# A decoder trunk's attention stage: weight fetches moved a step ahead, stores and reloads on GpSimd's queue, key halves in one transfer, one projection block kept for the last norm

## The chip, the cores and the metric

The kernel runs on one core of one Trainium2 chip. The metric is the device time of one execution in microseconds, the lower the better. All inputs lie in the chip's memory (HBM) when it starts; the result is written there.

## The reference

A trunk of two layers on one sequence of 1024 tokens with 1024 channels: one mLSTM layer, then one differential-attention layer, each followed by a squared-ReLU MLP, with a final norm. The change touches only the attention layer:

```python
for blk in range(S // Q_BLOCK):                 # 8 query blocks of 128
    q0 = blk * Q_BLOCK
    kv_len = q0 + Q_BLOCK                       # causal: keys 0 .. kv_len
    s1 = einsum('bhqd,bhkd->bhqk', q1[:, :, q0:kv_len], k1[:, :, :kv_len])
    s2 = einsum('bhqd,bhkd->bhqk', q2[:, :, q0:kv_len], k2[:, :, :kv_len])
    p1 = softmax(where(mask, s1, -inf)); p2 = softmax(where(mask, s2, -inf))
    a = p1 - lam * p2
    outs.append(einsum('bhqk,bhkv->bhqv', a, v[:, :, :kv_len]))
o = concatenate(outs, axis=2)
o = rms_norm(o, subln_g, SUBLN_EPS) * (1 - lam_init)    # per head, 128 channels
x = x + g1 * (o.reshape(B, S, 1024) @ w_out)
```

There are 8 heads; each has two query and key vectors of 64 channels and one value of 128. Everything is float32; the kernel reaches that accuracy on TensorE by splitting each operand into a high and a low part (float32r) and adding three products.

## The kernel before

**Stages.** The program is straight-line. An mLSTM layer and its MLP come first; then the query and key projections (`rope_out`), which store the rotated queries to the DRAM tensor `qdr` and the keys to `kdr`, high and low parts apart. The attention stage follows, then the second half of the output projection, the second MLP and the final norm. Tokens are handled in two halves throughout: half 0 is tokens 0 to 511, half 1 the others.

**The attention stage.** A *unit* is one head and one query block. `jobs` lists runs of units: heads 0 to 4 with all 8 blocks, then heads 5, 6, 7 with blocks 0 to 3, then heads 5, 6, 7 with blocks 4 to 7. For each step `i` of the loop the program issues `scores` of unit i+2, `combine` of unit i, `values` of unit i-1, and, two steps after a head's half is complete, its `subnorm`. `scores` multiplies the queries by the keys' high part (`ka`, line 960) and low part (`kb`, line 961), adds the mask (962) and takes the exponential on ScalarE (970). `combine` forms p1 - lam p2, transposes it (987) and copies it back (988). `values` multiplies by `v` (1001).

**Loads of a job.** `load` (line 923 on) brings, for each of the head's two vectors, the queries (`q`), the keys' high part twice and the keys' low part twice: the 64 rows of a key are wanted on partitions 0 to 63 and again on 64 to 127, since the queries' high and low parts lie there one above the other. That is a loop over `dup` with two transfers of 64 rows per key tile. The tiles have two buffers each (`kp`, bufs=2), so a job's keys are loaded while the job before it is computed. `load_v` brings the values.

**Fill work.** While the attention runs, other matmuls fill TensorE. `chunks` projects the values of heads 2 to 7 in three chunks (`token_steps`, lines 253 to 269, 8 steps each, with weights `w_vb` fetched and split into high and low at the chunk's start); `v_store` copies each step's result to `sv` and stores every second step to `vdr`. `goal(i)` says how many steps must have been issued by step i. `project_a` does the output projection of half 0 in 8 blocks (weights `w_do`, residual from `xdr`), one block per loop step after the last head's half 0 is normed. The sub-norm's results go straight into `yh` and `yl` where these are free; before that they are stored to `odr` and brought back by `reload`.

**What sets the order.** A scheduler orders each engine's instructions from the program's order and its own estimate of when each can run; `tc.issue_after` adds an edge on one engine. Each engine, SP included, runs its instructions strictly in order. Every DMA of the kernel is issued on SP's queue, so a transfer there also waits for whatever the transfers ahead of it wait for.

Of the kernel before, what the change touches and what calls it, by code (L numbers as in the profile page):

```python
# [17 lines left out]
P = 128  # L18
T = 1024
D = 1024  # L20
NB = D // P
# [3 lines left out]
NC = T // P  # L25
BH, BD, BV = 8, 64, 128
# [29 lines left out]
def tile_yoco(ctx: ExitStack, tc: tile.TileContext, x, c, pos, cst, vec, bg, lp, ada,  # L56
              w_in, w_v0, w_v, w_o, w_mo, w_kv, w_vb, w_q, w_do, w_up, w_dn, out):
    nc = tc.nc
    pe, act, dve, sp = nc.tensor, nc.scalar, nc.vector, nc.sync
# [15 lines left out]
    def f32(ap):  # L75
        return ap.bitcast(F32)
# [13 lines left out]
    yh = ctile([P, 2, NB, HT], "yh", F32R)  # L90
    yl = ctile([P, 2, NB, HT], "yl", F32R)
# [5 lines left out]
    kdr = dr.tile([2, 2 * BH, BD, T], F32, tag="kdr", name="kdr")  # L97
    qdr = dr.tile([2 * BH, 2, BD, T], F32, tag="qdr", name="qdr")
    odr = dr.tile([2, BH, 2, P, HT], F32, tag="odr", name="odr")
# [74 lines left out]
    def wfetch(src, shape):  # L174
        r = wp.tile(shape, F32, tag="w", name="wraw")
        sp.dma_start(out=r, in_=src)
        return r

    def wload(src, shape, nbg=1, pool=None, r=None, hpool=None):
        if r is None:  # L180
            r = wfetch(src, shape)
        h = (pool or hpool or wp).tile(shape, F32R, tag="w", name="wh")
        l = (pool or wp).tile(shape, F32R, tag="w", name="wl")
        split(h, l, r)
        bgwork(nbg)
        return h, l
# [63 lines left out]
                        if after and idx[-1] == n - 1 and (gi, h) in after:  # L250
                            after[gi, h]()

    def token_steps(src, w, consume, nbg=1, hook=None):
        ws = [wload(src[j], [P, 4, w], nbg) for j in range(2)]
        for tb in range(NC):
            ps = gps()[:, :w]
            half, o = tb // 4, (tb % 4) * P
            for k in range(NB):
                wh, wl = ws[k // 4]
                a, b = yh[:, half, k, o:o + P], yl[:, half, k, o:o + P]  # L260
                pe.matmul(ps, lhsT=a, rhs=wh[:, k % 4], start=k == 0, stop=False)  # L261
                pe.matmul(ps, lhsT=a, rhs=wl[:, k % 4], start=False, stop=False)  # L262
                pe.matmul(ps, lhsT=b, rhs=wh[:, k % 4], start=False, stop=k == NB - 1)  # L263
            consume(tb, ps)
            yield
            if tb == 3 and hook:
                hook()
# [562 lines left out]
    def rope_out(dst, scale):  # L830
# [31 lines left out]
                    store(g + i, ps, scale)  # L862
        return f

    def v_store(cc, scr):
        held = [None]

        def f(tb, ps):
            if tb % 2 == 0:
                held[0] = scr.tile([P, 2, 2, BV], F32, tag="sv", name="sv")  # L870
            v = held[0]
            act.copy(out=v[:, :, tb % 2], in_=ps.rearrange("p (h v) -> p h v", h=2))  # L872
            if tb % 2:
                for j in range(2):
                    sp.dma_start(out=vdr[2 * cc + j, :, tb - 1:tb + 1], in_=v[:, j])
        return f

    neg = scr.tile([P, P], F32, tag="neg", name="neg", bufs=1)
# [38 lines left out]
    with ExitStack() as ph:  # L917
# [7 lines left out]
        def load(h, b0, b1):  # L925
            ka, kb, qs = [], [], []
            qt, kt = slice(b0 * P, b1 * P), slice(0, b1 * P)
            for f in range(2):
                g = 2 * h + f
                a = kp.tile([P, T], F32R, tag=f"ka{f}", name="ka")  # L930
                b = kp.tile([P, T], F32R, tag=f"kb{f}", name="kb")
                q = kp.tile([P, T], F32R, tag=f"q{f}", name="q")
                sp.dma_start(out=f32(q[:, qt]), in_=qdr[g, :, :, qt].rearrange("s d t -> (s d) t"))
                for s, t in ((0, a), (1, b)):
                    for dup in range(2):
                        sp.dma_start(out=f32(t[dup * BD:dup * BD + BD, kt]), in_=kdr[s, g, :, kt])
                ka.append(a)
                kb.append(b)
                qs.append(q)
            heads[h] = dict(ka=ka, kb=kb, qs=qs)  # L940
# [67 lines left out]
        def subnorm(direct, h, half, o32, ss, ls):  # L1008
            v = ap_.tile([P, 4], F32, tag="v", name="v")
            dve.scalar_tensor_tensor(v, ls[:, 0], SUB_EPS, ls[:, 0], ALU.mult, ALU.mult)  # L1010
            dve.scalar_tensor_tensor(v, ss, 1.0 / BV, v, ALU.mult, ALU.add)
            r = rstd_small(ap_, v, 4)
            dve.tensor_tensor(out=o32, in0=o32, in1=r.unsqueeze(2).to_broadcast([P, 4, BV]), op=ALU.mult)
            ps = pt.tile([P, HT], F32, tag="tp", name="rps")
            for qb in range(4):
                pe.transpose(ps[:, qb * P:qb * P + P], o32[:, qb], ident)
            if direct:
                act.mul(out=yh[:, half, h], in_=ps, mul=gsub)
                dve.scalar_tensor_tensor(yl[:, half, h], ps, gsub, f32(yh[:, half, h]), ALU.mult, ALU.subtract)  # L1019
                return  # L1020
            oh = ap_.tile([P, HT], F32R, tag="ot", name="oh", bufs=2)
            ol = ap_.tile([P, HT], F32R, tag="ot", name="ol", bufs=2)
            act.mul(out=oh, in_=ps, mul=gsub)
            dve.scalar_tensor_tensor(ol, ps, gsub, f32(oh), ALU.mult, ALU.subtract)
            for j, t in enumerate((oh, ol)):
                sp.dma_start(out=odr[half, h, j], in_=f32(t))

        def reload(half, h):
            for j, t in enumerate((yh, yl)):
                sp.dma_start(out=f32(t[:, half, h]), in_=odr[half, h, j])  # L1030

        def chunks():
            for cc in range(1, 4):
                yield from token_steps(w_vb[cc], 256, v_store(cc, ap_))

        def project_a():
            raws = ahead + [wfetch(w_do[1], [P, NB, P])]
            nxt = wload(None, [P, NB, P], 0, r=raws[0])
            for nb in range(NB):
                wh, wl = nxt  # L1040
                if nb + 2 < NB:
                    raws.append(wfetch(w_do[nb + 2], [P, NB, P]))
                xs = ap_.tile([P, HT], F32, tag="ot", name="xs", bufs=2)
                sp.dma_start(out=xs, in_=xdr[:, 0, nb])
                ps = gps()
                for k in range(NB):
                    mm3(ps, wh[:, k], wl[:, k], yhk(0, k), ylk(0, k), k == 0, k == NB - 1)
                    if k == NB // 2 and nb + 1 < NB:
                        nxt = wload(None, [P, NB, P], 0, r=raws[nb + 1])
                dve.scalar_tensor_tensor(xs, ps, mcol(1, 2, nb), xs, ALU.mult, ALU.add)  # L1050
                sp.dma_start(out=xdr[:, 0, nb], in_=xs)
                if nb == 0:
                    act.activation(acc[0], xs, AF.Square)
                else:
                    s = ap_.tile([P, HT], F32, tag="ot", name="xq", bufs=2)
                    act.activation(s, xs, AF.Square)
                    dve.tensor_tensor(out=acc[0], in0=acc[0], in1=s, op=ALU.add)
                yield
# [16 lines left out]
                    return g0 + (g1 - g0) * (i - i0) // (i1 - i0)  # L1075
            return due[-1][1]

        norms, back, begun, ahead = [], ([], []), [], []
        fill, proj, done = chunks(), project_a(), FILL0
        load(*jobs[0])  # L1080
        load_v(*jobs[0])
# [5 lines left out]
        for i in range(len(seq) + 2 + LAG):  # L1087
            while done < goal(i):
                next(fill, None)
                done += 1  # L1090
                if done == ready[1] - 3:
                    ahead.append(wfetch(w_do[0], [P, NB, P]))
                if done == ready[1]:
                    for _ in fill:
                        pass
            if i in v_at:
                load_v(*v_at[i])
            for half in range(2):
                if back[half] and done >= ready[half]:
                    reload(*back[half].pop(0))  # L1100
            if i in load_at:
                load(*load_at[i])
            if i + AHEAD < len(seq):
                scores(*seq[i + AHEAD])
            if i < len(seq):
                combine(*seq[i])
            while norms and norms[0][0] < i - LAG:
                h, half = norms[0][1:3]
                direct = done >= ready[half]
                subnorm(direct, *norms.pop(0)[1:])  # L1110
                if not direct:
                    back[half].append((half, h))
                if (h, half) == (BH - 1, 0):
                    begun.append(i)
            if 0 < i <= len(seq):
                h, qb = seq[i - 1]
                r = values(h, qb)
                if r:
                    norms.append((i, h, qb // 4) + r)
            if begun and i > begun[0] and not back[0]:  # L1120
                next(proj, None)
        while back[1]:
            reload(*back[1].pop(0))
        for _ in proj:
# [129 lines left out]
```

## Time and profile before

| what | before |
| --- | --- |
| median of 3 runs | 2420.73 us (2416.79 to 2422.91) |
| the profiled execution | 2419.79 us |
| its span | 2418.0 us |
| TensorE (PE) busy | 98% of the span |
| attention stage | 1331 to 1678 us |
| mean granted TensorE clock | 0.994 |

A page of the profile lists busy time by engine, the span in slices, the DMA queues, the chain of work that ended last, the costliest groups and the DMA issues. In a timeline row the columns are start (us), length (us), engine, line, operation, what it writes and reads, and in brackets the idle time before it and what ended that. SPq is SP's queue of DMA issues: the length there is the time that SP needs to issue the transfer, not the transfer's own. In the list of DMA issues the columns are what is moved, how often, the size of each, and the median time from issue to landing. In a table of windows the columns are the stretch, its length, busy time and instruction count of PE, PEld, DVE, ACT and POOL, the granted clock, the mean busy share of the 16 DMA engines, and GB/s.

### The profile page before, as it was taken

The numbers are of one execution on the slowest core, as the hardware profiler recorded it, in microseconds if no ns is written. First come the engines' busy times: TensorE is split into PE (matmuls) and PEld (weight loads), VectorE is DVE, ScalarE is ACT, GpSimd is POOL, SyncE is SP. The second block draws the span as 40 slices with busy tenths as digits, with TensorE's granted clock in tenths as the row PEclk, the third lists the DMA queues.
The fourth block names the chain that finished last, engine by engine and source line by source line (L and its number), as shares of the span: only waits on it lengthen the run. The fifth ranks groups of instructions, "written<-read, shape, count | busy, mean of one in ns | idle before, by whom it ended". The sixth has DMA issues, their size and how long they took to land.

```text
span 2418.0 us, 30720 instructions
## 1 busy us (share of the span) xinstructions
PE 2358.6 (98%) x12018; PEld 1977.4 (82%) x12018; DVE 1548.5 (64%) x2552; ACT 976.8 (40%) x1874; POOL 0.2 (0%) x4
## 2 busy tenths in 40 slices
PE   7999999999999999999999999989999999999997
PEld 4899998778888888887788899977778888888886
DVE  7426544787877787775653477764776567566646
ACT  4324633444323323433332477754433323432332
POOL 0000000000000000000000000000000000000000
PEclk9999999999999999999999999999999999999999
DMA  7312242313422431341644754764111111111121
GB/s 307 121 57 84 71 157 79 122 44 127 135 91 84 131 130 56 116 143 49 205 144 138 220 150 153 222 193 165 57 61 36 57 61 44 40 61 57 36 70 70
DMA packets 110237, 262.60 MB, mean 109 GB/s; under 512 B 11658, under 2 KB 46986, under 8 KB 108300
## 3 DMA queue, kind: packets, MB, share of 16 engines
q1 hardware_dynamic: 110092, 260.65, 33.4%
q8 instruction: 94, 1.54, 0.3%
q14 instruction: 51, 0.42, 0.1%
HBM read 223.83 MB, written 36.77 MB: 108 GB/s over the span
## 4 chain that ended last, share of the span: by engine, by line
PE 91%; DMA 4%; DVE 2%; ACT 2%; issue 0%; SPq 0%; DVEq 0%; ACTq 0%
PE gps L189 24%; PE gps L191 24%; PE gps L190 24%; PE gps L261 3%; PE gps L262 3%; PE gps L263 3%; PE gps L1001 2%; PE sc L960 1%; PE sc L961 1%; PE tps L987 1%; DMA kb<-kdr 1%; DMA ka<-kdr 1%; DMA wraw<-in_w_vb_dram 1%; DVE adar L342 1%; PE hps L534 1%; PE hps L536 1%
## 5 line engine op out<-in xcount | busy, mean ns | idle before, releaser
L189 PE MATMUL gps<-yh,wh 128*128 128x512 f32 x1664 | 654.6, 397 | 4.2 <-DVE yl L1019 1.6
L190 PE MATMUL gps<-yl,wh 128*128 128x512 f32 x1664 | 658.3, 396 | 0.3 <-DVE yl L308 0.3
L191 PE MATMUL gps<-yh,wl 128*128 128x512 f32 x1664 | 655.3, 395 | 2.4 <-DVE wl L172 2.4
L189 PEld LDWEIGHTS gps<-yh,wh 128*128 128x128 f32 x1664 | 312.8, 188 | 82.0 <-ACT wh L171 1.8
L191 PEld LDWEIGHTS gps<-yh,wl 128*128 128x128 f32 x1664 | 312.9, 188 | 79.6 <-DVE wl L172 3.3
L190 PEld LDWEIGHTS gps<-yl,wh 128*128 128x128 f32 x1664 | 312.9, 188 | 75.7 <-issue 1.0
L681 DVE SCALAR_TENSOR_TENSOR x<-gps,mod,x 128x512 f32<-128x512 f32 x392 | 286.6, 747 | 51.4 <-PE gps L191 49.8
L171 ACT CAST wh<-wraw 128x1024 fp32r<-128x1024 f32 (+1 forms) x144 | 150.9, 1049 | 401.6 <-DMA wraw<-in_w_up_dram 192.6
L172 DVE TENSOR_TENSOR wl<-wraw,wh 128x1024 fp32r<-128x1024 f32 (+1 forms) x144 | 176.2, 1224 | 174.6 <-ACT wh L171 139.0
L261 PE MATMUL gps<-wh,yh 128*128 128x256 f32 (+1 forms) x768 | 222.9, 290 | 5.0 <-ACT sv L872 3.6
L262 PE MATMUL gps<-wl,yh 128*128 128x256 f32 (+1 forms) x768 | 219.0, 285 | 0.0
L263 PE MATMUL gps<-wh,yl 128*128 128x256 f32 (+1 forms) x768 | 218.3, 284 | 0.0
L171 ACT CAST eh<-e 128x1024 fp32r<-128x1024 f32 x56 | 58.8, 1049 | 242.8 <-DVE e L662 242.8
L151 DVE CUSTOM_DVE_ANT_0 adar<-adar,sil 128x1024 f32<-128x1024 f32 x96 | 117.0, 1222 | 54.6 <-DMA adar<-in_ada_dram 54.5
L261 PEld LDWEIGHTS gps<-wh,yh 128*128 128x128 f32 x768 | 144.8, 189 | 6.9 <-ACT sv L872 3.9
L262 PEld LDWEIGHTS gps<-wl,yh 128*128 128x128 f32 x768 | 144.9, 189 | 1.0
L263 PEld LDWEIGHTS gps<-wh,yl 128*128 128x128 f32 x768 | 144.9, 189 | 0.7
L619 ACT ACTIVATE b<-gps 128x512 f32<-128x512 f32 x112 | 66.9, 597 | 182.0 <-PE gps L191 176.9
L970 ACT ACTIVATE pf<-sc,mx 128x256 f32<-128x256 f32 (+7 forms) x128 | 95.3, 750 | 16.5 <-DVE mx L964 9.1
L172 DVE TENSOR_TENSOR el<-e,eh 128x1024 fp32r<-128x1024 f32 x56 | 68.4, 1222 | 46.8 <-PE gps L190 44.6
L189 PE MATMUL gps<-th,lh 128*128 128x512 f32 x224 | 88.9, 397 | 0.5 <-DVE x L681 0.5
L191 PE MATMUL gps<-th,ll 128*128 128x512 f32 x224 | 88.5, 395 | 0.0
(259 smaller groups left out, 3850.4 us busy)
## 6 DMA issues: line engine op xcount, KB each, us to landing
adar<-in_ada_dram SPq DMA_DIRECT2D x112, 512.0 KB, 4.2
wraw<-in_w_up_dram SPq DMA_DIRECT2D x64, 512.0 KB, 3.3
e<-in_w_dn_dram SPq DMA_DIRECT2D x56, 256.0 KB, 3.1
m<-in_w_dn_dram SPq DMA_DIRECT2D x56, 256.0 KB, 3.1
x<-in_x_dram SPq DMA_DIRECT2D x8, 1024.0 KB, 8.8
wraw<-in_w_mo_dram SPq DMA_DIRECT2D x16, 512.0 KB, 3.2
ka<-kdr SPq DMA_DIRECT2D x32, 256.0 KB, 7.9
kb<-kdr SPq DMA_DIRECT2D x32, 256.0 KB, 7.3
```

The source lines that it names most:

```text
L151: dve.tensor_tensor_reduce(r, r, sil, 1.0, 0.0, ALU.mult, ALU.add, mod[:, n:n + 1])
L171: act.copy(out=ph, in_=src)
L172: dve.tensor_tensor(out=pl, in0=src, in1=f32(ph), op=ALU.subtract)
L189: pe.matmul(ps, lhsT=wh, rhs=a, start=first, stop=False, skip_group_check=more)
L190: pe.matmul(ps, lhsT=wh, rhs=b, start=False, stop=False, skip_group_check=more)
L191: pe.matmul(ps, lhsT=wl, rhs=a, start=False, stop=last, skip_group_check=more)
L261: pe.matmul(ps, lhsT=a, rhs=wh[:, k % 4], start=k == 0, stop=False)
L262: pe.matmul(ps, lhsT=a, rhs=wl[:, k % 4], start=False, stop=False)
L263: pe.matmul(ps, lhsT=b, rhs=wh[:, k % 4], start=False, stop=k == NB - 1)
L619: act.activation(dst, ps, AF.Relu)
L681: dve.scalar_tensor_tensor(xs, ps, mcol(l, 5, nb), xs, ALU.mult, ALU.add)
L970: act.activation(pf[f][:, 0:n * P], pp[f][:, 0:n * P], AF.Exp, bias=mx[:, f:f + 1], accum_out=ls[:, f, qb % 4:qb % 4 + 1])
```

## The change

Four edits, all in the attention stage:

- **Weights a step sooner.** `token_steps` can be given its weights. `chunks` now fetches the next chunk's two weight tiles after step 3 of the present chunk (`tb == NC - 5`) and splits them after step 6. The second output weight tile, which `project_a` fetched when it began, is fetched when the last chunk ends.
- **Stores and reloads on GpSimd's queue.** The stores to `vdr` and `odr` and the reloads from `odr` are issued by GpSimd instead of SP; the reloads come behind the last store of values issued by then.
- **Key halves in one transfer.** One DMA of 128 rows whose source is read twice (`partition_broadcast(2)`) takes the place of two DMAs of 64 rows.
- **One block kept.** Of the 8 blocks of `project_a` the loop issues 7 as before, and the eighth only after the last unit.

```diff
-    def token_steps(src, w, consume, nbg=1, hook=None):
-        ws = [wload(src[j], [P, 4, w], nbg) for j in range(2)]
+    def token_steps(src, w, consume, nbg=1, hook=None, ws=None):
+        if ws is None:
+            ws = [wload(src[j], [P, 4, w], nbg) for j in range(2)]
...
-                    sp.dma_start(out=vdr[2 * cc + j, :, tb - 1:tb + 1], in_=v[:, j])
+                    stored[0] = nc.gpsimd.dma_start(out=vdr[2 * cc + j, :, tb - 1:tb + 1], in_=v[:, j])
...
                 for s, t in ((0, a), (1, b)):
-                    for dup in range(2):
-                        sp.dma_start(out=f32(t[dup * BD:dup * BD + BD, kt]), in_=kdr[s, g, :, kt])
+                    sp.dma_start(out=f32(t[:, kt]), in_=kdr[s, g, :, kt].partition_broadcast(2))
...
-                sp.dma_start(out=odr[half, h, j], in_=f32(t))
+                nc.gpsimd.dma_start(out=odr[half, h, j], in_=f32(t))
 
         def reload(half, h):
-            for j, t in enumerate((yh, yl)):
-                sp.dma_start(out=f32(t[:, half, h]), in_=odr[half, h, j])
+            with tc.issue_after(stored[0].ins):
+                for j, t in enumerate((yh, yl)):
+                    nc.gpsimd.dma_start(out=f32(t[:, half, h]), in_=odr[half, h, j])
 
         def chunks():
+            raws = chunk_raws(1)
+            nxt = chunk_halves(raws)
             for cc in range(1, 4):
-                yield from token_steps(w_vb[cc], 256, v_store(cc, ap_))
+                for tb, _ in enumerate(token_steps(None, 256, v_store(cc, ap_), ws=nxt)):
+                    if cc < 3 and tb == NC - 5:
+                        raws = chunk_raws(cc + 1)
+                    if cc < 3 and tb == NC - 2:
+                        nxt = chunk_halves(raws)
+                    yield
+
+        def chunk_raws(cc):
+            return [wfetch(w_vb[cc][j], [P, 4, 256]) for j in range(2)]
+
+        def chunk_halves(raws):
+            return [wload(None, [P, 4, 256], 0, r=r) for r in raws]
 
         def project_a():
-            raws = ahead + [wfetch(w_do[1], [P, NB, P])]
+            raws = list(ahead)
...
                     for _ in fill:
                         pass
+                    ahead.append(wfetch(w_do[1], [P, NB, P]))
...
-            if begun and i > begun[0] and not back[0]:
-                next(proj, None)
+            if begun and i > begun[0] and not back[0] and (len(steps) < NB - 1 or i > len(seq)):
+                steps.append(next(proj, None))
```

How the instructions stand now, at three places. First SP's queue where the attention stage begins: keys of heads 0 and 1, value weights, stores of values (`vdr<-sv`) and the values of heads 0 and 1. Before:

```order
L176 DMA wraw<-in_w_vb_dram 128x1024
L936 DMA ka<-kdr 64x1024 x2
L875 DMA vdr<-sv 128x256 x2
L936 DMA ka<-kdr 64x1024 x3
L936 DMA kb<-kdr 64x1024 x4
L875 DMA vdr<-sv 128x256 x2
L936 DMA ka<-kdr 64x1024
L936 DMA kb<-kdr 64x1024 x2
L936 DMA ka<-kdr 64x1024 x2
L936 DMA kb<-kdr 64x1024
L875 DMA vdr<-sv 128x256 x2
```

The same place in the changed kernel, up to the keys of head 2:

```order
L176 DMA wraw<-in_w_vb_dram 128x1024
L938 DMA ka<-kdr 128x1x1024 x4
L938 DMA kb<-kdr 128x1x1024 x4
L176 DMA wraw<-in_w_vb_dram 128x1024
L946 DMA v<-vdr 128x1024 x2
L176 DMA wraw<-in_w_vb_dram 128x1024
L938 DMA ka<-kdr 128x1x1024
```

The stores are gone from SP's queue, and 16 key loads have become 8 of twice the size; everything behind them on SP, the next weights and both heads' values among it, still stands behind all of them.

Second, SP's queue where the output projection of half 0 begins: residual blocks (`xs`), keys, queries and values of heads 6 and 7, reloads (`yh`, `yl`), and the output weights (`in_w_do`). Before:

```order
L1030 DMA yl<-odr 128x512
L933 DMA q<-qdr 128x512
L875 DMA vdr<-sv 128x256 x2
L936 DMA ka<-kdr 64x1024 x2
L936 DMA kb<-kdr 64x1024 x2
L933 DMA q<-qdr 128x512
L944 DMA v<-vdr 128x1024
L936 DMA ka<-kdr 64x1024 x2
L936 DMA kb<-kdr 64x1024 x2
L176 DMA wraw<-in_w_do_dram 128x1024
```

Now:

```order
L1060 DMA xs<-xdr 128x512 x2
L176 DMA wraw<-in_w_do_dram 128x1024
L938 DMA ka<-kdr 128x1x1024
L936 DMA q<-qdr 128x512
L938 DMA kb<-kdr 128x1x1024
L938 DMA ka<-kdr 128x1x1024
L936 DMA q<-qdr 128x512
L938 DMA kb<-kdr 128x1x1024
L176 DMA wraw<-in_w_do_dram 128x1024
L946 DMA v<-vdr 128x1024 x2
```

The fetch that stood behind the last head's keys now stands ahead of them, and no store or reload is between.

Third, TensorE at the stage's end: the last values (`gps<-v,at`), the mean square of half 0 (`nps<-acc`), and the last norm's transposes (`rps`). Before:

```order
L1001 MATMUL gps<-v,at 128x128 x8
L288 MATMUL nps<-acc,one 128x512
L1016 MATMUL rps<-cs,o_14320 128x128 x4
L189 MATMUL gps<-yh,wh 128x512
```

Now the last values and the first rows of the kept block, which is followed, 24 matmuls later, by the last norm's transposes:

```order
L1018 MATMUL rps<-cs,o_13919 128x128 x4
L1003 MATMUL gps<-v,at 128x128 x8
L189 MATMUL gps<-yh,wh 128x512
L190 MATMUL gps<-yl,wh 128x512
L191 MATMUL gps<-yh,wl 128x512
```

The block of the projection has moved from ahead of the last values to the place between them and the last norm.

More of the change, by code (lines that the diff above doesn't have):

```diff
@@ L863, in rope_out @@
         return f
+    stored = [None]
     def v_store(cc, scr):
@@ L1076, in goal @@
             return due[-1][1]
-        norms, back, begun, ahead = [], ([], []), [], []
+        norms, back, begun, ahead, steps = [], ([], []), [], [], []
         fill, proj, done = chunks(), project_a(), FILL0
```

## The prediction

> **What bounds the kernel now.** I read the page's totals first, then the table of windows for the stage that the diff touches, then TensorE's own waits in that stage, and last the chain of waits behind the longest of them.
>
> ```profile
> span 2418.0 us, 30720 instructions
> PE 2358.6 (98%) x12018; PEld 1977.4 (82%) x12018; DVE 1548.5 (64%) x2552; ACT 976.8 (40%) x1874; POOL 0.2 (0%) x4
> ```
> ```profile
> core 0: us, PE busy (x) PEld busy (x) DVE busy (x) ACT busy (x) POOL busy (x), PEclk, DMA share, GB/s
> 1331.00:1600.00 269.00, 256.43 (x2001) 244.74 (x1999) 174.61 (x359) 174.52 (x555) 0.00 (x0) 1.00 0.67 194
> 1331.00:1678.00 347.00, 326.45 (x2385) 304.16 (x2384) 219.74 (x431) 214.89 (x648) 0.00 (x0) 0.99 0.61 181
> ```
>
> TensorE sets the time. The attention stage runs from 1331 to 1678, and in its 347 us TensorE is idle for 347.00 - 326.45 = 20.6 us. That is all that better fetching can win there, 0.85% of the span. GpSimd does nothing in the stage. The waits of TensorE between 1331 and 1678 (total, times, longest) say what the idle time is:
>
> ```profile
> PE tps L987 <- ACT at L988: 9.3, 3, 7.5
> PE gps L261 <- ACT sv L872: 3.6, 2, 2.4
> PE sc L961 <- DMA kb<-kdr: 2.1, 2, 1.7
> PE gps L189 <- DVE yl L1019: 1.6, 1, 1.6
> PE nps L288 <- DVE v L1011: 1.1, 1, 1.1
> PE rps L1016 <- DVE o L1013: 0.7, 1, 0.7
> PE gps L1001 <- DMA v<-vdr: 0.5, 1, 0.5
> ```
>
> The largest, 7.5 us, is not ScalarE being slow. ScalarE's timeline shows it standing in front of a cast for weights that had not landed, and the copy that TensorE needs is behind that cast; the second row is the stage's end, where nothing is left to lay beside the last norm:
>
> ```profile
> 1603.09 1.04 ACT L171 CAST wh<-wraw 128x1024 fp32r<-128x1024 f32 x1 [13.53 <-DMA wraw<-in_w_do_dram]
> ```
> ```profile
> 1677.76 0.50 PE L189 MATMUL gps<-yh,wh 128*128 128x512 f32 x1 [1.56 <-DVE yl L1019]
> ```
>
> **Key halves in one transfer: the part that decides.** The list of DMA issues gives the key loads of before: 64 of 256 KB and 24 of 128 KB. SP's timeline gives the first, the last, and the first load for each of five heads that follow one another:
>
> ```profile
> ka<-kdr SPq DMA_DIRECT2D x32, 256.0 KB, 7.9
> kb<-kdr SPq DMA_DIRECT2D x32, 256.0 KB, 7.3
> ka<-kdr SPq DMA_DIRECT2D x12, 128.0 KB, 3.1
> kb<-kdr SPq DMA_DIRECT2D x12, 128.0 KB, 3.2
> pi<-in_pos_dram SPq DMA_DIRECT2D x1, 32.0 KB
> tdr<-sin SPq DMA_DIRECT2D x1, 32.0 KB, 1.4
> ```
> ```profile
> 1334.88 1.14 SPq L936 DMA_DIRECT2D ka<-kdr  x2
> 1380.05 0.45 SPq L936 DMA_DIRECT2D ka<-kdr  x1
> 1518.35 0.45 SPq L936 DMA_DIRECT2D ka<-kdr  x1
> 1592.22 1.23 SPq L936 DMA_DIRECT2D kb<-kdr  x2
> ```
>
> After the change there are 32 of 512 KB and 12 of 256 KB, 38 full ones by bytes. Their source now begins with a dimension of two copies, and the question is over how many of the 16 DMA engines such a transfer is spread. No key load of before has that form. One other transfer does: the positions (pi) are read with eight copies in front, 128 rows of 256 B. The stores of the rotary tables (tdr) move the same 32 KB in 128 rows of 256 B, with 128 in front on both sides. Both run with next to nothing else in flight, so the share of busy DMA engines can be compared, 0.02 us at a time:
>
> ```profile
> 74.24:74.26 0.02, 0.02 (x1) 0.00 (x0) 0.00 (x0) 0.02 (x1) 0.00 (x0) 1.00 1.19 269
> 74.99:75.01 0.02, 0.02 (x2) 0.02 (x1) 0.00 (x0) 0.02 (x1) 0.00 (x0) 1.00 1.15 269
> 51.64:51.66 0.02, 0.02 (x1) 0.02 (x1) 0.02 (x1) 0.00 (x0) 0.00 (x0) 1.00 0.72 157
> 51.74:51.76 0.02, 0.02 (x1) 0.02 (x2) 0.02 (x1) 0.00 (x0) 0.00 (x0) 1.00 0.68 154
> 51.50:51.55 0.05, 0.00 (x0) 0.00 (x0) 0.05 (x1) 0.05 (x1) 0.00 (x0) 1.00 0.07 3
> ```
>
> The tables peak at 1.19 and 1.15 (packets overlap within an engine, so the share passes 1). The positions stand flat near 0.70 and never rise above 0.72, with about 0.07 of it there before they begin. 0.63 is half of 1.17: eight copies in front look like eight engines. By the same reading two copies in front are two engines, and all key loads share these two.
>
> The Trainium skill states this as a rule, on its page "DMA: Bandwidth & Descriptors", sections "Why a DMA increments its semaphore by 16 and not by 1" and "Rules for kernel authors": the outermost dimension limits the engines, and a leading broadcast of c copies keeps a DMA on at most c of them, the lowest-numbered ones. By it the time comes out as below; the trace agrees for c = 8 (0.72 against 1.19), and no run here shows c = 2. The same section of rules also says that two transfers to the two halves of the partitions should be one of 128 partitions; by that alone the change would gain (the first rival).
>
> What one engine moves is bounded by three windows, of x at the start, of a 128-partition weight load, and of key loads:
>
> ```profile
> 8.00:44.00 36.00, 28.33 (x68) 14.95 (x69) 28.39 (x54) 19.37 (x30) 0.00 (x0) 0.91 1.02 414
> 1152.00:1156.00 4.00, 3.83 (x17) 2.80 (x16) 2.16 (x3) 1.65 (x2) 0.00 (x0) 1.00 1.04 444
> 1384.00:1392.00 8.00, 8.00 (x71) 8.00 (x71) 5.50 (x14) 5.55 (x19) 0.00 (x0) 1.00 1.04 266
> ```
>
> 414/16 = 25.9 GB/s an engine over 36 us, at most 444/16 = 27.8, at least 266/16 = 16.6. I take 25.9: the new loads fill 128 partitions as x does, and the longest window is the steadiest. A full load puts 262,144 B on each of two engines, 10.1 us, and the 38 of them need 385 us. The rest of the stage's traffic crosses these engines too: 194 GB/s x 269 us = 52.2 MB, less 19.9 MB of keys, is 32.3 MB, 2.0 MB an engine, 78 us. A head asks for four loads, 40 us and about 10 us of the rest, where the heads followed each other every (1518.35 - 1380.05)/4 = 34.6 us: the two engines become the bound, and two sets of key buffers let the next head's loads queue without a gap. I add 10 us for two gaps (while the first head is computed, and in the short heads). The last keys land at 1335 + 385 + 78 + 10 = 1808.
>
> Before, they were issued at 1592 and landed, at a median of 7.3 us, near 1601; 77 us later the stage was over. Of these the 7.5 us wait and the 3.4 us of the last three waits (1.6, 1.1, 0.7) go, so 66 us remain: 1874 instead of 1678, **+196 us**. With 27.8 GB/s and the rest of the traffic costing nothing it is 1335 + 359 + 66 = 1760, +82; with 16.6 it is 1335 + 600 + 122 + 66 = 2123, +445.
>
> **The other parts.** *Weights a step sooner*: the chunk's fetches and the output weights are queued on SP ahead of loads they used to follow. Their prize is 7.5 us and some of the first 3.6 us; on the two-engine path I count nothing beyond the 7.5 already taken, since what SP issues sooner still waits behind keys in the same two engines. *Stores and reloads on GpSimd's queue*: 32 + 20 + 20 = 72 issues leave SP. The trace shows no GpSimd DMA. From one side SP only gains its 72 x 0.32 us (the shortest issue of a store, the list's first 320 ns), 23 us of an engine that is not the bound; from the other, if GpSimd took a store's landing (6.5 us median) for each, 72 x 6.5 = 468 us, longer than the stage.
>
> ```profile
> vdr<-sv SPq DMA_DIRECT2D x32, 128.0 KB, 6.5
> ```
> ```profile
> L875 SPq DMA_DIRECT2D vdr<-sv x32: 320/351/1102, 1336.1 to 1582.4; - x32
> ```
>
> I take nothing, being nearer to SP's issue time; GpSimd is idle and nothing but stores and reloads is queued on it. If that cover fails, ScalarE's copies into sv wait, and behind them the exponentials. *One block kept*: 24 matmuls move behind the last norm; they cover the three last waits, the 3.4 us counted above. Late next is the mean square of that block, which TensorE meets only after another block.
>
> **Sum.** The profiled execution took 2419.8 us (its span 2418.0), 0.9 us below the median of 2420.7. 2419.8 + 196 = 2616.
>
> **Rivals.** (1) *The transfer spreads over all 16 engines: faster.* For it: one load of 128 partitions could run like x (414 GB/s) rather than like today's half loads (266). Against it: the positions' flat 0.7. It decides at (34.6 - 10)/4 = 6.1 us a load, which 3.3 engines at 25.9 GB/s reach; from four up the loads hide as they do now. Then 7.5 + 3.6 + 2.1 + 0.5 + 3.4 go, and 1.4 of the rest of the first row: 18.5 us, **2401**. (2) *Two engines at the rate of today's key loads*, 16.6 GB/s: **2865**. For it: two engines fetch the same rows. Against it: those windows had 16 engines at work on 64 partitions. (3) *GpSimd's queue is the bound*, keys spread: 468 us of queue from 1336 on end at 1804, where the stage ended at 1678: +126, **2546**. Nothing in the trace speaks for it but its silence. (4) *No change*: spread, with the 20 us given back to later DMA waits, 2420.
>
> **Chances.** Two engines at about 26 GB/s 0.70; (2) 0.13; (1) 0.12; (3) 0.03; (4) 0.02. So slower by over 0.3% 0.86, within 0.3% (about what a measurement of this kernel can tell from no change) 0.02, faster 0.12. The range leaves (1) and the far end of (2) out: 2520 to 2840, the low end near the +82 with some of the traffic counted, the high end short of +445.
>
> **What would show it.** Right: key loads that land after 10 us and more, most of them far later; a DMA share of 0.2 to 0.3 between 1400 and 1750 and about 80 to 130 GB/s; TensorE's waits led by scores on ka and kb; heads 45 to 55 us apart; the last block of projection between the last values and the norm. Wrong: key loads that land in 4 to 8 us with the share near 1 would mean that they spread, and rival (1). Stores on GpSimd's queue that land late while sv waits would mean (3).

## The result, and the profile after

The changed kernel takes 2687.55 us (median of 5 runs, 2685.72 to 2690.23) where the kernel before took 2421.64 in the same comparison: ratio 1.1109, 95% interval 1.1097 to 1.1121. That is 266 us more. The forecast was 196 us more, 2616, within a range of 2520 to 2840.

The page of the changed kernel opens with its span and TensorE's totals:

```profile
span 2685.8 us, 30721 instructions
PE 2385.3 (89%) x12018; PEld 2003.7 (75%) x12018; DVE 1548.4 (58%) x2552; ACT 980.8 (37%) x1874; POOL 39.3 (1%) x76
```

The span grew by 2685.8 - 2418.0 = 267.8 us. All but 1 us of it lies in the attention stage, which now ends at 1944.55, where it ended at 1677.76. The table of windows for the stage, with a window in which only key loads move and two in which nothing does (columns as before; the last three are granted clock, DMA share and GB/s):

```profile
1331.00:1945.00 614.00, 354.19 (x2386) 330.47 (x2385) 219.67 (x432) 217.50 (x648) 39.08 (x72) 0.78 0.30 104
1359.00:1391.00 32.00, 0.00 (x0) 0.00 (x0) 0.00 (x0) 0.00 (x0) 0.00 (x0) 0.52 0.13 53
1433.00:1449.00 16.00, 13.79 (x92) 12.11 (x92) 14.13 (x31) 13.58 (x47) 0.00 (x0) 1.00 0.01 2
1657.00:1661.00 4.00, 4.00 (x35) 3.88 (x34) 2.16 (x5) 3.38 (x11) 0.00 (x0) 1.00 0.00 0
```

The second row is the answer in one line. For 32 us no engine computes, and the 16 DMA engines are busy to 0.13 of their time, which is 2/16 = 0.125, moving 53 GB/s: two engines at 26 GB/s each. The trace has no row for a single engine, so this and the counts of engines below are read from shares and rates. The first row splits the loss: TensorE's idle time rose from 20.6 us to 614.00 - 354.19 = 259.8, by 239 us, and its busy time from 326.45 to 354.19, by 28 us, for the same matmuls, at a mean granted clock of 0.78 where it was 0.99.

The chain of waits at the stage's start shows SP itself held up; a row is start, length and what the chain ran through:

```profile
1334.96 0.56 SPq L938
...
1335.57 1.50 SPq L938
...
1337.12 10.75 SPq L938
...
1347.91 11.01 SPq L938
...
1359.02 10.25 SPq L938
...
1369.32 9.76 SPq L938
...
1379.12 9.78 SPq L938
...
1388.95 9.78 SPq L938
...
1398.83 26.66 DMA wraw<-in_w_vb_dram
```

The first two issues take 0.56 and 1.50 us; from the third on, each holds SP for about 10 us. The mean of the last six is 10.2 us, close to the time of one load at 53 GB/s, 524,288 / 53e3 = 9.9 us: SP goes on at the pace of the loads. Only then is the weight fetch issued that TensorE's fill work needs. TensorE's waits in the stage (total, times, longest), and four casts for weights in ScalarE's timeline:

```profile
PE sc L963 <- DMA kb<-kdr: 77.8, 6, 34.1
PE gps L1003 <- DMA v<-vdr: 58.3, 4, 26.6
PE sc L962 <- ACT pf L972: 41.3, 6, 21.7
PE gps L262 <- ACT sv L875: 34.2, 2, 33.8
PE tps L989 <- ACT at L990: 32.5, 2, 32.0
PE sc L962 <- DMA ka<-kdr: 11.2, 2, 6.5
PE gps L189 <- DVE yl L1021: 2.4, 1, 2.4
```
```profile
1425.51 1.05 ACT L171 CAST wh<-wraw 128x1024 fp32r<-128x1024 f32 x1 [73.28 <-DMA wraw<-in_w_vb_dram]
1546.89 1.05 ACT L171 CAST wh<-wraw 128x1024 fp32r<-128x1024 f32 x1 [35.05 <-DMA wraw<-in_w_vb_dram]
1645.47 1.05 ACT L171 CAST wh<-wraw 128x1024 fp32r<-128x1024 f32 x1 [19.21 <-DMA wraw<-in_w_do_dram]
1829.19 1.05 ACT L171 CAST wh<-wraw 128x1024 fp32r<-128x1024 f32 x1 [21.70 <-DMA wraw<-in_w_do_dram]
```

Only 89 of these 260 us name the keys. The values (58.3) and the weights stand behind keys, on SP and in the two engines; and the rows that name ScalarE are nearly all ScalarE standing in front of a cast for weights, as it did once before the change: TensorE's waits of 33.8, 32.0, 17.3 and 21.7 us, 105 of the 108 in these rows, each end 1 to 3 us after one of the four casts began.

### The profile page after: what moved, and what is told of

Its sections match the earlier page's. It is cut to its first block, busy times and chain, and to the rows that moved or that the text cites. A ratio compares the mean times of both kernels' runs of the same rounds, so it can differ in the third digit from the quotient of the medians.

```text
span 2685.8 us, 30721 instructions
## 1 busy us (share of the span) xinstructions
PE 2385.3 (89%) x12018; PEld 2003.7 (75%) x12018; DVE 1548.4 (58%) x2552; ACT 980.8 (37%) x1874; POOL 39.3 (1%) x76
## 4 chain that ended last, share of the span: by engine, by line
PE 73%; DMA 11%; SPq 3%; DVE 2%; ACT 1%; issue 0%; DVEq 0%; ACTq 0%
PE gps L189 21%; PE gps L190 21%; PE gps L191 21%; DMA kb<-kdr 4%; SPq L938 3%; DMA v<-vdr 2%; PE gps L1003 2%; DMA wraw<-in_w_vb_dram 2%; PE gps L262 2%; PE gps L263 2%; PE gps L264 2%; DMA wraw<-in_w_do_dram 2%; PE sc L962 1%; PE sc L963 1%; PE tps L989 1%; SPq L176 0%
## 5 line engine op out<-in xcount | busy, mean ns | idle before, releaser
L262 PEld LDWEIGHTS gps<-wh,yh 128*128 128x128 f32 x768 | 149.0, 194 | 37.5 <-ACT sv L875 34.6
L1003 PE MATMUL gps<-v,at 128*128 128x128 f32 x576 | 87.6, 296 | 58.3 <-DMA v<-vdr 58.3
L963 PE MATMUL sc<-kb,q 128*128 128x512 f32 (+2 forms) x192 | 69.4, 372 | 77.8 <-DMA kb<-kdr 77.8
L962 PE MATMUL sc<-ka,q 128*128 128x512 f32 (+2 forms) x192 | 77.3, 403 | 54.6 <-ACT pf L972 41.3
L1003 PEld LDWEIGHTS gps<-v,at 128*128 128x128 f32 x576 | 79.2, 209 | 59.6 <-issue 32.2
```

The lines of the kernel that those rows point to most:

```text
L962: lead[0] = pe.matmul(ps[:, k0:k1], lhsT=lq, rhs=H["ka"][f][:, k0:k1], start=True, stop=False)
L1003: pe.matmul(ps, lhsT=at[:, k], rhs=H["v"][:, k], start=k == 0, stop=k == n - 1)
```

## The experiments

Those whose name begins with a_ start from the changed kernel, those with b_ from the kernel before. The kernels of before that ran beside them had medians of 2418.0 to 2419.2.

### Key halves apart again (a_two_halves)

```diff
-                    sp.dma_start(out=f32(t[:, kt]), in_=kdr[s, g, :, kt].partition_broadcast(2))
+                    for dup in range(2):
+                        sp.dma_start(out=f32(t[dup * BD:dup * BD + BD, kt]), in_=kdr[s, g, :, kt])
```

> The changed kernel with the key loads as two transfers of 64 rows again; the other three edits stay. If the two copies in front of the source hold each key load to two DMA engines (my theory), the 266 us go with them and the rest of the change shows its own gain: 2401 to 2421, key loads landing in 7 to 8 us. If GpSimd's queue or the earlier weight fetches were what delays the stage, it stays above 2500. If the loss had two causes, it lands between.

Measured: 2413.24 us, ratio to before 0.9980 (0.9971 to 0.9990). The whole loss is in this one edit, and the three others together gain 0.2%.

### The key edit alone (b_keys_only)

The edit above the other way round, in the kernel before.

> The kernel before with the one-transfer key loads alone. By my theory it has the whole loss: 2680 to 2760, rather more than the 2688 of the changed kernel, since the stores of values and the weight fetches now also queue on SP behind the key loads. If GpSimd's queue is the cause: 2410 to 2430.

Measured: 2705.4 us, ratio 1.1188 (1.1172 to 1.1204). It carries the loss, and 18 us more. Where these come from was not taken apart. One of ScalarE's waits stands here and not in the changed kernel: the stores are on SP, behind the keys, and the copies into sv wait for a store to land:

```profile
ACT sv L872 <- DMA vdr<-sv: 78.6, 2, 59.6
```

### The same transfer with the copies behind (a_interleaved)

```diff
-                sp.dma_start(out=f32(q[:, qt]), in_=qdr[g, :, :, qt].rearrange("s d t -> (s d) t"))
+                sp.dma_start(out=f32(q[:, qt]), in_=qdr[g, :, :, qt].rearrange("s d t -> d s t"))
...
-                    sp.dma_start(out=f32(t[:, kt]), in_=kdr[s, g, :, kt].partition_broadcast(2))
+                    src = kdr[s, g, :, kt]
+                    sp.dma_start(out=f32(t[:, kt]), in_=src.unsqueeze(1).broadcast_to([BD, 2, b1 * P]))
```

The sum over partitions in `scores` does not care in which order the channels lie, as long as queries and keys agree. So the partitions can hold channel 0 twice, then channel 1 twice, and the source begins with 64 channels instead of 2 copies.

> The changed kernel, still with one transfer of 128 rows for each key tile and the same bytes, but with the two copies behind the 64 channels in the source (the partitions hold channel 0 twice, channel 1 twice, and so on, the queries to match). By my theory the leading dimension of 64 lets it use all 16 engines: 2395 to 2421, a load in 2.5 to 8 us. If reading each row twice in one transfer, or the size of 512 KB, is what costs, it stays near 2690.

Measured: 2407.67 us, ratio 0.9959 (0.9944 to 0.9974): one transfer instead of two, every row still read twice, the same bytes, and it has the lowest median of the study. The window in which the first key loads run, and the list of DMA issues:

```profile
1338.00:1352.00 14.00, 14.00 (x120) 14.00 (x120) 0.00 (x0) 2.59 (x6) 2.15 (x4) 1.00 1.02 409
```
```profile
ka<-kdr SPq DMA_DIRECT2D x16, 512.0 KB, 7.3
kb<-kdr SPq DMA_DIRECT2D x16, 512.0 KB, 8.2
```

All engines are busy, at 409 GB/s, and a full load lands after 7.3 to 8.2 us although eight or four are issued together. Neither reading a row twice nor the size was the cost.

### How many copies stand in front (a_four_copies, a_eight_copies, a_four_last, a_sixteen_last)

```diff
-kdr[s, g, :, kt].partition_broadcast(2)
+kdr[s, g, :BD // 2, kt].partition_broadcast(4)
+kdr[s, g, :BD // 4, kt].partition_broadcast(8)
+kdr[s, g, BD - P // 4:, kt].partition_broadcast(4)
+kdr[s, g, BD - P // 16:, kt].partition_broadcast(16)
```

The four new lines belong to the four kernels of the heading, in their order. Each loads as many bytes as the changed kernel, but leaves out channels: the scores are those of a half, a quarter, a half and an eighth of a key's channels.

> The changed kernel with each key load reading half of the key's rows (32 channels) four times instead of all 64 twice, so that the scores are those of half the channels: same bytes written, same partitions, same order on PE, ACT, DVE and POOL. By my theory it uses four engines: 10.2 / 2 = 5.1 us a load, 20 us for a head's four and some 5 us of the rest, below the 34.6 us in which TensorE needs them, so the loss nearly goes: 2400 to 2460. If reading a row several times is what costs, it is no faster than 2690. If the spread has nothing to do with the number of copies, 2690.

> The changed kernel with each key load reading a quarter of the key's rows (16 channels) eight times, so that the scores are those of a quarter of the channels; same bytes written, same order on PE, ACT, DVE and POOL. By my theory eight engines: two copies took 10.2 us a load, four took 5.4, so 2.7 us here; the 35 us at the stage's start, where the weights stand behind eight key loads, should shrink to some 10 us or nothing: 2405 to 2440. If it is the number of reads of a row that costs, it is slower than the 2521 of four copies.

> As with four copies, but of the last 32 channels of a key, not the first: these come from the stores that the whole key waits for, so that SP's queue too stands exactly as in the changed kernel (with the first 32 it did not: both value weights stood behind the first eight key loads). 5.4 us a load. If the 100 us that four copies still lost were mostly those weights at the stage's start (35 us of TensorE's waits, and the clock that fell with them), this takes 2430 to 2490. If four engines are too few whatever the order, about 2520.

> The last 8 channels of a key read sixteen times (the scores are those of an eighth of the channels), with the order on PE, ACT, DVE, POOL and SP exactly as in the changed kernel. If the number of copies in front is the number of engines, all 16 work and the loss is gone with nothing else changed: 2400 to 2420. If reading the same rows often costs, or the order is part of the loss, above 2450.

| copies in front | kernel | median us | ratio to before (95%) |
| --- | --- | --- | --- |
| 2 | the changed kernel | 2687.55 | 1.1109 (1.1097 to 1.1121) |
| 4, first channels | a_four_copies | 2520.80 | 1.0424 (1.0409 to 1.0439) |
| 4, last channels | a_four_last | 2518.45 | 1.0419 (1.0405 to 1.0433) |
| 8, first channels | a_eight_copies | 2464.34 | 1.0186 (1.0169 to 1.0202) |
| 16, last channels | a_sixteen_last | 2417.65 | 0.9989 (0.9978 to 1.0000) |

The first channels of a key are stored before the last ones, so in a_four_copies and a_eight_copies the loads may start sooner, and both value weights came to stand behind the first eight key loads on SP. With the last channels every engine's order, SP's too, is that of the changed kernel, and only the number of copies differs. Windows in which the key loads are nearly alone, of a_four_last (first), a_eight_copies and a_sixteen_last:

```profile
1356.00:1362.00 6.00, 2.99 (x26) 2.84 (x24) 0.00 (x0) 0.00 (x0) 0.00 (x0) 1.00 0.25 104
```
```profile
1359.00:1369.00 10.00, 0.00 (x0) 0.00 (x0) 0.00 (x0) 0.00 (x0) 0.00 (x0) 0.50 0.51 189
```
```profile
1338.00:1352.00 14.00, 14.00 (x121) 14.00 (x119) 0.00 (x0) 2.65 (x6) 2.15 (x4) 1.00 1.03 311
```

With the 0.13 of the changed kernel this is 2/16, 4/16, 8/16 and all: the share of busy engines is the number of copies in front. The rate does not grow as evenly: 53/2, 104/4, 189/8 and 311/16 are 26, 26, 24 and 19 GB/s an engine, where the interleaved form reached 409/16 = 26; the cause of this is open. At 26 GB/s an engine, four carry a load in 524,288 / 104e3 = 5.0 us.

Four and eight copies missed what was expected, and in the same way. At 5.0 us a load four engines were expected to keep up (below 2460), and eight to lose nothing much (below 2440); they lost 4.2% and 1.9%. The order of the weights was not the reason: with it restored, 2430 to 2490 was expected if it was, and about 2520 if four engines are too few whatever the order, and both kinds of four agree within 3 us. TensorE's waits in a_four_last, two further windows of it, and a row each of SP's and ScalarE's timelines show where the time went:

```profile
PE gps L1003 <- DMA v<-vdr: 25.2, 3, 13.1
PE sc L962 <- ACT pf L972: 22.5, 6, 11.5
PE gps L262 <- ACT sv L875: 20.5, 2, 20.0
PE sc L963 <- DMA kb<-kdr: 17.3, 3, 10.7
PE tps L989 <- ACT at L990: 17.2, 2, 16.7
```
```profile
1372.00:1378.00 6.00, 0.00 (x0) 0.00 (x0) 0.00 (x0) 0.00 (x0) 0.00 (x0) 0.50 1.02 246
1380.00:1390.00 10.00, 0.00 (x0) 0.00 (x0) 0.00 (x0) 1.00 (x2) 0.00 (x0) 0.50 0.25 104
```
```profile
1365.69 5.70 SPq L176 DMA_DIRECT2D wraw<-in_w_vb_dram  x1
```
```profile
1389.00 1.04 ACT L171 CAST wh<-wraw 128x1024 fp32r<-128x1024 f32 x1 [36.06 <-DMA wraw<-in_w_vb_dram]
```

Most of it is not a wait for keys at all. SP issued the second weights at 1365.69 and the values behind them. From 1372 to 1378 all engines are busy; from 1380 to 1390 the share is back at 0.25, while ScalarE waits for these weights until 1389.00. The reading that fits: a weight fetch is spread over all 16 engines and is complete only when the slowest has done its part, and four of them still have keys ahead of it. The trace has no row for a single engine, so this is read from the shares.

### Key loads on GpSimd's queue (a_keys_gp)

```diff
-                    sp.dma_start(out=f32(t[:, kt]), in_=kdr[s, g, :, kt].partition_broadcast(2))
+                    nc.gpsimd.dma_start(out=f32(t[:, kt]), in_=kdr[s, g, :, kt].partition_broadcast(2))
```

Stores and reloads go back to SP, so that GpSimd issues keys alone.

> The changed kernel with the one-transfer key loads alone on GpSimd's queue, stores and reloads on SP again: weights, values and queries no longer stand behind keys in one queue. If the two engines' throughput is the bound, as the forecast's sum had it, little changes: 2640 to 2690. If the loss beyond it comes from weights and values that stand behind keys in SP's queue, 2560 to 2630. If it is SP's queue that does not spread them and GpSimd's does, about 2415.

Measured: 2460.81 us, ratio 1.0179 (1.0165 to 1.0193), outside of all three. The list of DMA issues, the line of its queue on the page, and a window with one head's four loads in flight:

```profile
ka<-kdr POOLq DMA_DIRECT2D x16, 512.0 KB, 22.3
kb<-kdr POOLq DMA_DIRECT2D x16, 512.0 KB, 22.4
```
```profile
q0 software_dynamic: 39616, 20.08, 3.6%
```
```profile
1392.00:1404.00 12.00, 12.00 (x99) 11.65 (x97) 8.51 (x23) 8.62 (x31) 0.00 (x0) 1.00 0.61 215
```

With four or more in flight a load lands 22 us after its issue (the median), in packets of 20.08 MB / 39,616 = 507 B, where SP's queue brought one load every 10.2 us and so four in 41. The four together keep 0.61 of the engines busy, not 0.13: more than two engines are at work, so the loads do not all share the same two as they do on SP's queue. The Trainium skill, page "DMA: Bandwidth & Descriptors", section "Why a DMA increments its semaphore by 16 and not by 1", says that SP's queue takes the lowest-numbered engines and GpSimd's as many consecutive ones from a cursor that moves on. By that rule four loads on two engines each would be an estimated share of 0.5, and the 0.61 measured, with other traffic in the same window, agrees. That it is the cursor, and what keeps a load at 22 us, no run here shows. The run therefore does not tell the two engines' throughput from SP's order, as it was meant to.

### The other edits alone, and the interleaved form alone

b_queue_only, b_sooner_only and b_last_only each put one of the other edits of the diff into the kernel before; b_interleaved puts the edit of a_interleaved there in place of the two transfers of 64 rows.

> The kernel before with the stores and reloads on GpSimd's queue alone. The forecast counted nothing for it: 2413 to 2423 (the run of before gave 2418). If GpSimd takes long over a store, slower than 2430; if the loads on SP come sooner without the stores between, some of the 2.1 + 0.5 us of waits for kb and v and the 3.6 us for sv go: about 2412.

> The kernel before with the weights fetched a step sooner alone. The forecast had 7.5 us of waits at the cast of the output weights and part of the 3.6 us at the stage's start: 2408 to 2413. If the weights only push the keys of the last heads back, 2418.

> The kernel before with the last projection block kept for the last norm alone. The forecast had the three last waits gone, 3.4 us: 2414 to 2416. The trace of the changed kernel still shows one of 2.4 us for yl behind the last norm: then about 1 us, 2417, which this number of rounds can hardly tell from 2418.

> The kernel before with only the one-transfer key loads in the interleaved form (the 64 channels in front, the two copies behind). Of the gain of 0.41% that this form had with the other three edits, those three alone had about 0.2%: so some 0.2% here, 2411 to 2417, if the two add up; 2408 if it carries the gain alone.

| kernel | median us | ratio to before (95%) |
| --- | --- | --- |
| b_queue_only | 2415.30 | 0.9986 (0.9975 to 0.9997) |
| b_sooner_only | 2416.30 | 0.9992 (0.9982 to 1.0002) |
| b_last_only | 2416.89 | 0.9989 (0.9980 to 0.9998) |
| b_interleaved | 2409.78 | 0.9966 (0.9954 to 0.9979) |

Each of the three measured some 2 to 4 us faster, and none is worth more than 6 by its interval; b_sooner_only, for which 2408 to 2413 had been expected, cannot be told from no change. The interleaved form alone brings 0.34%, more than expected, and with the three others on top 0.41%; the intervals overlap, so that the three still add something there is not shown. In b_sooner_only the cast that waited 13.53 us for the output weights still waits, in ScalarE's timeline, and so does TensorE behind it; in b_last_only the wait behind the last norm is the one of the changed kernel:

```profile
1596.75 1.04 ACT L171 CAST wh<-wraw 128x1024 fp32r<-128x1024 f32 x1 [9.46 <-DMA wraw<-in_w_do_dram]
```
```profile
PE tps L990 <- ACT at L991: 4.8, 3, 3.4
```
```profile
PE gps L189 <- DVE yl L1022: 2.4, 1, 2.4
```

## Why the prediction was right, point by point

**Two copies, two engines.** Shown, as far as shares can show it: the flat 0.13, the series 2, 4, 8, 16, and the interleaved form, in which the same two copies of the same rows cost nothing once they stand behind the channels. The positions' share of 0.72 had been read as eight engines, 0.63 being taken for half of 1.17 (it is 0.54 of it); eight copies of keys stand at 0.51.

**What one engine moves.** 25.9 GB/s was taken, 53/2 = 26.5 measured; 10.1 us a load was forecast, 10.2 measured. The lower bound of 16.6 GB/s, from which the rival of 2865 came, is out.

**The sum came 70 us short**: stage end 1874 forecast, 1944.6 measured. The step that failed is "two sets of key buffers let the next head's loads queue without a gap", with its 10 us for two gaps. The chain's row for the last head's values shows when the backlog was gone, and SP's waits show what made the gaps:

```profile
1857.46 18.02 DMA v<-vdr
```
```profile
SPq L938 <- PE sc L964: 76.4, 5, 21.5
```

From 1335 to 1875 are 540 us. The loads take 38 x 10.2 = 388 of them. In windows of 1 us the DMA share is below 0.10 for 49 us in all, 19 between 1425 and 1452, 14 between 1545 and 1575 and 16 between 1640 and 1675 (parts of them are the two windows without traffic shown first): there a head's loads cannot start, since TensorE has not yet finished with the buffers, and TensorE is late, as its waits are read above, because it had waited for keys, and for the weights and values behind them. So the two engines and TensorE hold each other up in turn, and the gaps are 49 us, not 10. What is left, 540 - 388 - 49 = 103 us, stands where 78 had been put for the rest of the traffic; these 25 us were not taken apart. Behind 1875 came 69 us to the end of the stage, where 66 had been taken. Together 3 + 39 + 25 + 3 = 70 us.

**What the trace was to show.** Between 1400 and 1750 the DMA share is 0.28 and the rate 98 GB/s, as forecast (0.2 to 0.3, 80 to 130). For the key loads the page has no time to landing; what stands for it is SP's 10 us an issue. Heads were to be 45 to 55 us apart. The first loads of heads 2 to 5 on SP:

```profile
1449.52 0.50 SPq L938 DMA_DIRECT2D ka<-kdr  x1
...
1484.25 1.72 SPq L938 DMA_DIRECT2D ka<-kdr  x1
...
1569.92 0.49 SPq L938 DMA_DIRECT2D ka<-kdr  x1
...
1602.03 4.28 SPq L938 DMA_DIRECT2D ka<-kdr  x1
```

They are 34.7, 85.7 and 32.1 us apart. Only the mean, 50.8, lies in the forecast's band, in part by luck: loads without a gap had been forecast, and the trace has two heads close together and then a wait for buffers, whose 20 us the mean takes in.

Scores on kb do lead TensorE's waits. But more of them together are for values, and for ScalarE behind a cast of weights, than for keys.

**Rival (1) had a wrong condition.** "From four up the loads hide as they do now" compared a head's load time with the time TensorE takes for a head, 34.6 us. Four engines met it and lost 100 us, eight lost 45: as the waits are read above, what decides is not only whether the keys keep up, but how long everything else waits behind them when eight are issued at once. With all engines its time was 2401; of its 18.5 us a_two_halves reached 5.0 (2418.21 - 2413.24) and a_interleaved 10.5.

**The small terms.** *Weights a step sooner*: 7.5 us had been taken off the path behind the last keys; alone the edit gained 2 to 3 us, if anything, and the wait at TensorE fell to 3.4. *One block kept*: the 3.4 us of three waits became one of 2.4; the kept block's matmuls run ahead of the last norm's transposes, and none is left to lie behind them. *Stores and reloads on GpSimd's queue*, counted at nothing: 0.14% gained alone; and the rival of 468 us of queue is out. These errors, a few us each, vanish beside 266.

## What to carry to other kernels

Before two transfers are joined into one, look at which dimension comes first in the new source: a broadcast of two in front left this kernel two DMA engines of sixteen, and the same bytes with the copies behind the rows left it all of them. A flat DMA share at a fraction like 0.13, 0.25 or 0.5 over a stretch in which transfers are waited for is the sign. Then ask not only whether the slow transfers keep up on average, but what is queued behind their largest burst: four engines had throughput enough here, and still cost 4%.

## What the runs showed of the hardware that had not been expected

- At the stage's start SP issued two of these loads in 0.56 and 1.50 us and was then held for 9.8 to 11.0 us at each further one: a slow transfer held up the issue of everything behind it.
- On GpSimd's queue the same transfer went in packets of 507 B and landed 22 us after its issue, but four in flight kept 0.61 of the engines busy, where SP's queue kept 0.13 and brought one every 10.2 us.
- The granted clock fell to 0.50 to 0.52 in the long waits and averaged 0.78 over the stage, where it had been 0.99; the stage's matmuls were busy for 354 us instead of 326.
